# A three-layer transformer on one core: the same program, put in order by another timing model

## The chip, the core and the metric

The kernel runs on one core of a Trainium2 chip. The metric is the device time of one execution in microseconds, lower is better. The core has five engines that work side by side, each on a queue of its own in a fixed order: TensorE (PE for its matmuls, PEld for its weight loads), VectorE (DVE), ScalarE (ACT), GpSimd (POOL) and SyncE (SP), which here only issues transfers.

## What is computed

Three layers run one after the other over 256 tokens of width 1024, all in float32. The first two share a frame and differ in the mixer; the third has a mixer of three parts:

```
for i in range(2):
    x = x + 0.5 * swiglu(rms_norm(x, g[0]), w_gate, w_up, w_down)      # 1024 -> 2816 -> 1024
    x = x + mixer_i(rms_norm(x, g[1]))       # i = 0: gated spatial mixing + a chunked recurrence
                                             # i = 1: attention with low-rank q and k, v (8 heads)
    x = x + 0.5 * swiglu(rms_norm(x, g[2]), w_gate, w_up, w_down)
    x = x + rms_norm(sigmoid(rms_norm(x, g[3]) @ w_gate) * (p_i @ w_proj), g[4])   # embedding layer
x = x + concat(attention, state_space, pooling)(rmsnorm(x)) @ w_out     # hybrid layer
x = x + swiglu(rmsnorm(x), w_gate, w_up, w_down)
return rmsnorm(x)
```

## The kernel before

Activations lie with features on the partitions and the 256 tokens along the free axis; a weight is the stationary operand, 128 by 128, and the activations stream past it in 256 columns. Some products (`tm`) go the other way round, with tokens on the output's partitions and weights as the moving operand, up to 512 columns wide.

A float32 product is made of three passes: every operand is split into a high part in the type that TensorE takes at full pace and a low part, the rest, and high times high, low times high and high times low add up in PSUM. Weights come from HBM packed in pieces of 2048 columns (1 MB), in the order in which the program uses them. `load_piece` (L225) has SP load a piece into one of three buffers, then splits each half of it: ScalarE copies it to `whi` (L248) and VectorE subtracts that from the raw weights into `wlo` (L249). There are six buffers for each of the two parts, so splits can run three pieces ahead. There are 440 pairs of such instructions. All matmuls go through `mm` (L163), so the profile shows nearly all of TensorE under one line.

The program in the order of its stages: `ffn` (the swiglu layers, five of them), `even`, `ple` (the embedding layer, twice), `mla` (attention), `hybrid`, and a last normalization. A normalization needs a sum over features, a matmul with ones (`Stat.begin`), a few tiny VectorE steps (`rsqrt`) and a broadcast by matmul (`Stat.finish`). In `ple` it comes twice: the second one, `now()`, has to be through before the next layer's inputs exist. Behind the first embedding layer, `fill` puts the projection for the second one (`ple_proj`) into that place; behind the second, `fill` is None.

Python only traces the instructions. When the `TileContext` closes, a scheduler puts them in order: it plays the program through on a model of the machine's timing, and whenever an engine is free in that model, gives it the first instruction in program order among those whose inputs and buffers are there by the model's clock. It also hands out the buffers and places all semaphores. The kernel's text steers it in two ways: `high_priority()` moves a block ahead, and `behind(ins)` (the context's `issue_after`) has a block's instructions queued behind a given one on the same engine:

```
m = self.marks if self.hold == 0 else (None, None)
if self.hold == -1:
    m = None, self.rsq
if (self.piece, h) == self.late[0]:
    m = None, self.late[1]
with self.behind(m[0]), self.behind(m[1]):
    nc.scalar.activation(hi[:, i], s, AF.Copy)
    nc.vector.tensor_tensor(lo[:, i], s, hi[:, i].bitcast(FT), op=OP.subtract)
```

On the chip each engine then runs its queue in the order that was fixed at build time, whatever is ready.

In attention (`mla`), the lines that the prediction names: L1001 transposes the rotated key part, L1003 scales it by the keys' norm on VectorE, L936 transposes tiles back through PSUM (once from `big`, once from `o`). In `ple`, L82 and L500 are activations that need another function table than the one before.

Of the kernel before, what the change touches and what calls it, by code (L numbers as in the profile page):

```python
# [1614 lines left out]


def build(nc, a, at):
    with tile.TileContext(nc) as tc, ExitStack() as es:
        k = Kern(nc, tc, a, es, at)
        k.run()  # L1620
    return k.takes
# [19 lines left out]
```

## Time and profile before

| | |
|---|---|
| time, median of 3 runs | 1368.15 us (1366.81 to 1370.12) |
| the profiled execution's own time | 1364.73 us |
| its span, first to last instruction | 1363.0 us |
| instructions | 25969 |
| mean granted TensorE clock | 0.994 |

The profile is of one execution. A row of windows gives, for each engine, the busy time in that stretch and the number of instructions that started there, then the granted clock (1.00 is 2.4 GHz), the share of the DMA engines' time and the bandwidth. A row of the timeline gives start and length in us, engine, line and operands, and in brackets how long the engine sat idle before it and what ended that.

### The profile page before, as it was taken

What the parts mean: (1) busy time and instruction counts of PE and PEld (TensorE: products, weight loads), DVE (VectorE), ACT (ScalarE), POOL (GpSimd) and SP (SyncE); (2) the same over time, 40 slices, a digit from 0 to 9 for tenths busy, and PEclk for the clock granted to TensorE, in tenths of its full rate; (3) what the DMA queues carried; (4) which work ended last, traced back from release to release, by engine and by line L of the source; (5) the groups of instructions that cost most, each with busy time, mean ns of one, the idle gap of its engine ahead of it and who ended that gap; (6) DMA issues with size and microseconds to landing.
All of it is one profiled execution on the core that took longest, in us unless ns stands there. A gap on an engine that the chain in (4) does not pass through costs nothing.

```text
span 1363.0 us, 25969 instructions
## 1 busy us (share of the span) xinstructions
PE 1335.7 (98%) x10872; PEld 1304.9 (96%) x10872; DVE 920.0 (67%) x1527; ACT 726.8 (53%) x1110; POOL 78.3 (6%) x94
## 2 busy tenths in 40 slices
PE   8999999999999999999999899999998999999997
PEld 7999999999999999999999679999998988999997
DVE  6866657968666557866556767766558786766643
ACT  6554546646554456655445656544445665644442
POOL 3100010002000001000010002000001000200001
PEclk9999999999999999999999999999998999999998
DMA  9755555244555453555455323555554442555541
GB/s 323 244 185 183 171 201 173 90 174 168 200 188 203 160 203 138 200 190 188 166 194 193 108 90 132 184 188 188 180 185 156 155 149 100 181 190 187 185 158 60
DMA packets 34645, 235.50 MB, mean 173 GB/s; under 512 B 3984, under 2 KB 4496, under 8 KB 6880
## 3 DMA queue, kind: packets, MB, share of 16 engines
q1 hardware_dynamic: 32976, 230.24, 48.9%
q0 software_dynamic: 832, 2.47, 0.6%
q8 instruction: 85, 1.39, 0.4%
q10 hardware_dynamic: 720, 1.13, 0.2%
q14 instruction: 32, 0.26, 0.1%
HBM read 232.78 MB, written 1.05 MB: 172 GB/s over the span
## 4 chain that ended last, share of the span: by engine, by line
PE 75%; DVE 3%; ACT 2%; issue 1%; DVEq 0%; ACTq 0%
PE acc L163 70%; PE aux L163 5%; DVE wlo L249 1%; PE aux L1119 0%; ACT whi L248 0%; DVE big L1164 0%; DVE qs L950 0%; ACT at L1121 0%; DVE kv L950 0%; ACT ae L1111 0%; ACT big L938 0%; ACT big L1168 0%; DVE big L1486 0%; ACT gu L949 0%; PE aux L936 0%
## 5 line engine op out<-in xcount | busy, mean ns | idle before, releaser
L249 DVE TENSOR_TENSOR wlo<-wraw,whi 128x1024 fp32r<-128x1024 f32 (+1 forms) x440 | 530.8, 1220 | 271.8 <-ACT whi L248 179.8
L248 ACT ACTIVATE whi<-wraw 128x1024 fp32r<-128x1024 f32 (+1 forms) x440 | 451.1, 1047 | 329.0 <-PE acc L163 234.7
L163 PE MATMUL acc<-hh,whi 128*128 128x256 f32 x2192 | 335.0, 283 | 9.0 <-ACT whi L248 5.8
L163 PE MATMUL acc<-hl,whi 128*128 128x256 f32 x2192 | 333.9, 282 | 0.2 <-DVE hl L532 0.2
L163 PE MATMUL acc<-hh,wlo 128*128 128x256 f32 x2192 | 333.1, 282 | 0.7 <-DVE wlo L249 0.7
L163 PEld LDWEIGHTS acc<-hh,whi 128*128 128x128 f32 x2192 | 292.1, 190 | 9.7 <-ACT whi L248 5.8
L163 PEld LDWEIGHTS acc<-hh,wlo 128*128 128x128 f32 x2192 | 292.1, 189 | 1.5 <-DVE wlo L249 1.1
L163 PEld LDWEIGHTS acc<-hl,whi 128*128 128x128 f32 x2192 | 292.2, 189 | 0.4 <-DVE hl L532 0.4
L163 PE MATMUL acc<-big,whi 128*128 128x256 f32 x2032 | 276.1, 282 | 0.0
L163 PEld LDWEIGHTS acc<-big,whi 128*128 128x128 f32 x2032 | 259.7, 188 | 0.4 <-ACT big L259 0.2
L163 PE MATMUL acc<-big,wlo 128*128 128x256 f32 x1016 | 163.6, 282 | 0.0
L163 PEld LDWEIGHTS acc<-big,wlo 128*128 128x128 f32 x1016 | 138.9, 188 | 0.0
L307 POOL TENSOR_TENSOR sqa<-sqa,sq 128x256 f32<-128x256 f32 x72 | 64.0, 889 | 1148.1 <-ACT sq L306 1146.2
L418 DVE TENSOR_TENSOR gu<-acc,rb 128x512 f32<-128x512 f32 (+1 forms) x122 | 81.9, 678 | 56.3 <-PE acc L163 56.3
L262 ACT ACTIVATE hh<-x,cols 128x256 fp32r<-128x256 f32 x64 | 30.2, 503 | 85.2 <-DVE x L457 79.0
L259 ACT ACTIVATE big<-pr 128x256 fp32r<-128x256 f32 x114 | 46.0, 409 | 54.7 <-DVE pr L436 53.0
L434 ACT ACTIVATE sg<-gu 128x256 f32<-128x256 f32 x110 | 44.7, 411 | 37.4 <-DVE gu L418 37.4
L260 DVE TENSOR_TENSOR big<-pr,big 128x256 fp32r<-128x256 f32 x114 | 47.3, 420 | 20.5 <-ACT big L259 20.4
L436 DVE TENSOR_TENSOR pr<-sg,gu 128x256 f32<-128x256 f32 x110 | 45.3, 418 | 3.2 <-ACT sg L434 3.2
L263 DVE SCALAR_TENSOR_TENSOR hl<-x,cols,hh 128x256 fp32r<-128x256 f32 x64 | 37.8, 617 | 8.9 <-ACT hh L262 8.6
L163 PE MATMUL aux<-big 128*128 128x128 f32 (+5 forms) x260 | 39.3, 311 | 0.6 <-DVE big L672 0.6
L306 ACT ACTIVATE sq<-x 128x256 f32<-128x256 f32 x62 | 24.0, 405 | 24.5 <-DVE x L459 18.3
(294 smaller groups left out, 798.3 us busy)
## 6 DMA issues: line engine op xcount, KB each, us to landing
wraw<-wts SPq DMA_DIRECT2D x216, 1024.0 KB, 4.9
wraw<-wts SPq DMA_DIRECT2D x3, 512.0 KB, 8.3
x<-xT SPq DMA_DIRECT2D x3, 256.0 KB, 7.5
wraw<-wts SPq DMA_DIRECT2D x2, 256.0 KB, 3.9
big<-wsT POOLq DMA_DIRECT2D x1, 512.0 KB, 12.6
gu<-pT ACTq DMA_DIRECT2D x2, 256.0 KB, 2.9
out<-big SPq DMA_DIRECT2D x2, 256.0 KB, 2.2
out<-big ACTq DMA_DIRECT2D x2, 256.0 KB, 2.5
```

The lines of the kernel that those rows point to most:

```text
L163: return self.nc.tensor.matmul(out, l, r, start=start, stop=stop, skip_group_check=True).ins
L248: nc.scalar.activation(hi[:, i], s, AF.Copy)
L249: nc.vector.tensor_tensor(lo[:, i], s, hi[:, i].bitcast(FT), op=OP.subtract)
L259: a = nc.scalar.activation(hi, src, AF.Copy)
L260: b = nc.vector.tensor_tensor(lo, src, hi.bitcast(FT), op=OP.subtract)
L262: a = nc.scalar.activation(hi, src, AF.Copy, scale=scale)
L263: b = nc.vector.scalar_tensor_tensor(lo, src, scale, hi.bitcast(FT), op0=OP.mult, op1=OP.subtract)
L306: nc.scalar.activation(q, src, AF.Square)
L307: self.mark = nc.gpsimd.tensor_tensor(self.sq[0], self.sq[0], q, op=OP.add).ins
L418: self.nc.vector.tensor_tensor(out.rearrange("p (u t) -> p u t", u=n), ps.rearrange("p (u t) -> p u t", u=n), rb.unsqueeze(1).to_broadcast ...
L434: self.mark = nc.scalar.activation(sg, gu[:, :T], AF.Silu).ins
L436: nc.vector.tensor_tensor(pr, sg, gu[:, T:], op=OP.mult)
```

## The change

One argument is added where the context is opened. With it the scheduler plays the program through on the build's other timing model, which follows each instruction in more detail. The instructions traced, their priorities, the marks of `behind` and the buffers stay as they are; what may differ is the order in which each engine's queue is filled, and with it which buffer a tile gets and where the semaphores stand.

```
 def build(nc, a, at):
-    with tile.TileContext(nc) as tc, ExitStack() as es:
+    with tile.TileContext(nc, schedule_with_timeline_sim=True) as tc, ExitStack() as es:
         k = Kern(nc, tc, a, es, at)
         k.run()
     return k.takes
```

## Rows read from the trace of the kernel before

**Rows 1.** The page's first part: busy us (share of the span) xinstructions.
```profile
PE 1335.7 (98%) x10872; PEld 1304.9 (96%) x10872; DVE 920.0 (67%) x1527; ACT 726.8 (53%) x1110; POOL 78.3 (6%) x94
```

**Rows 2.** Chain that ended last: by engine (the page), by line (the chain's own view).
```profile
PE 75%; DVE 3%; ACT 2%; issue 1%; DVEq 0%; ACTq 0%
...
by line: PE acc L163 70.0%; PE aux L163 4.9%; DVE wlo L249 0.9%; issue 0.7%; PE aux L1119 0.4%; ACT whi L248 0.3%; DVE big L1164 0.3%; DVE qs L950 0.2%; ACT at L1121 0.2%; DVE kv L950 0.2%; ACT ae L1111 0.2%; ACT big L938 0.2%; ACT big L116
```

**Rows 3.** The page's costliest groups: busy us, mean ns | idle before, releaser.
```profile
L249 DVE TENSOR_TENSOR wlo<-wraw,whi 128x1024 fp32r<-128x1024 f32 (+1 forms) x440 | 530.8, 1220 | 271.8 <-ACT whi L248 179.8
L248 ACT ACTIVATE whi<-wraw 128x1024 fp32r<-128x1024 f32 (+1 forms) x440 | 451.1, 1047 | 329.0 <-PE acc L163 234.7
```

**Rows 4.** Windows by stage, the last one a part of 750:830.
```profile
0.00:25.00 25.00, 18.45 (x137) 18.03 (x138) 16.56 (x31) 15.88 (x30) 12.03 (x22) 1.00 0.87 313
25.00:200.00 175.00, 175.00 (x1468) 175.00 (x1467) 113.19 (x157) 89.15 (x126) 9.20 (x8) 1.00 0.59 201
200.00:300.00 100.00, 99.38 (x755) 93.49 (x754) 80.50 (x139) 57.19 (x74) 2.10 (x3) 1.00 0.45 157
300.00:525.00 225.00, 225.00 (x1910) 224.80 (x1909) 148.74 (x219) 118.91 (x173) 15.94 (x18) 1.00 0.54 185
525.00:550.00 25.00, 23.23 (x194) 22.83 (x193) 20.34 (x42) 16.83 (x33) 1.93 (x3) 1.00 0.25 86
550.00:725.00 175.00, 175.00 (x1488) 175.00 (x1487) 113.52 (x157) 89.18 (x125) 4.41 (x6) 1.00 0.56 193
...
750.00:830.00 80.00, 74.63 (x453) 60.81 (x452) 57.45 (x152) 50.10 (x98) 0.00 (x0) 1.00 0.28 97
830.00:1025.00 195.00, 195.00 (x1657) 194.93 (x1655) 127.75 (x178) 98.83 (x147) 12.59 (x14) 1.00 0.53 184
1025.00:1075.00 50.00, 46.10 (x365) 45.34 (x365) 39.87 (x84) 28.09 (x46) 5.33 (x5) 0.93 0.39 136
1075.00:1150.00 75.00, 74.59 (x551) 66.31 (x551) 60.18 (x158) 50.83 (x97) 0.00 (x0) 1.00 0.40 137
1150.00:1350.00 200.00, 200.00 (x1688) 199.94 (x1688) 121.28 (x168) 98.44 (x144) 12.60 (x13) 1.00 0.48 164
1350.00:1363.00 13.00, 4.27 (x30) 3.80 (x28) 3.73 (x13) 1.04 (x3) 1.41 (x2) 0.67 0.21 81
...
750.00:775.00 25.00, 20.86 (x98) 15.86 (x96) 23.87 (x60) 15.21 (x23) 0.00 (x0) 1.00 0.28 98
```

**Rows 5.** Windows of 5 us behind the second embedding layer.
```profile
1045.00:1050.00 5.00, 2.16 (x11) 1.79 (x12) 3.89 (x12) 1.76 (x6) 0.00 (x0) 0.73 0.57 192
1050.00:1055.00 5.00, 5.00 (x29) 5.00 (x27) 4.86 (x13) 3.27 (x10) 0.00 (x0) 0.59 0.04 18
...
1060.00:1065.00 5.00, 5.00 (x46) 5.00 (x44) 2.19 (x2) 1.76 (x2) 0.00 (x0) 1.00 0.35 95
```

**Rows 6.** Timeline of TensorE at the first embedding layer, of ScalarE at the second.
```profile
538.50 0.51 PE L163 MATMUL acc<-hh,whi 128*128 128x256 f32 x2 [1.57 <-ACT hh L527]
...
1031.87 1.28 ACT L500 ACT_TABLE_LOAD   x1
...
1033.16 1.16 ACT L500 ACTIVATE gu<-gu 128x512 f32<-128x512 f32 x2
```

**Rows 7.** Timeline of VectorE and TensorE in attention, 772 to 777 us.
```profile
773.11 0.38 PE L1001 MATMUL aux<-ident,big 128*128 128x128 f32 x2
773.16 1.22 DVE L249 TENSOR_TENSOR wlo<-wraw,whi 128x1024 fp32r<-128x1024 f32 x1
774.29 1.28 DVE L1003 TENSOR_TENSOR big<-aux,kfr 128x512 f32<-128x512 f32 x2
...
775.13 1.23 PE L936 MATMUL aux<-ident,big 128*128 128x128 f32 x8 [1.64 <-DVE big L1003]
...
776.19 1.04 PE L936 MATMUL aux<-ident,o 128*128 128x128 f32 x8
```

More of the change, by code (lines that the diff above doesn't have):

```diff
@@ L1617, in build @@
 def build(nc, a, at):
-    with tile.TileContext(nc) as tc, ExitStack() as es:
+    with tile.TileContext(nc, schedule_with_timeline_sim=True) as tc, ExitStack() as es:
         k = Kern(nc, tc, a, es, at)
```

## The prediction

> **What bounds the kernel now.** I read the page's engine totals first: TensorE is busy 1335.7 of 1363.0 us [rows 1]. The reader is to see that nothing else comes near it (VectorE is at 920, ScalarE at 727), so an order can only help or harm where TensorE waits. The chain that ended last says the same and names the others: 75% of the span runs through TensorE, 3% through VectorE, 2% through ScalarE, and 0.9% and 0.3% of it are the weight splits of L249 and L248 [rows 2], that is 12.3 and 4.1 us. One such split takes 1.22 us on VectorE and 1.05 us on ScalarE [rows 3], so some ten and four of the 440 pairs stand in that chain today.
>
> The windows by stage then show where TensorE waits [rows 4]. In five long stretches, 970 us together (25:200, 300:525, 550:725, 830:1025, 1150:1350), it is busy without a break; these are the swiglu layers, with VectorE at 61 to 66% and ScalarE at 49 to 53%. Its idle time is elsewhere: 6.55 us at the start, 8.73 at the end, and between them 0.62 in the even mixer (200:300), 1.77 at the first embedding layer (525:550), 5.37 in the attention mixer (750:830), 3.90 at the second embedding layer (1025:1075) and 0.41 in the hybrid layer (1075:1150). The inner five sum to 12.1 us.
>
> **The change part by part.** It adds no operation, removes none and resizes none: same matmuls, same splits, same transfers. What moves is the place of each instruction in its engine's queue. Three kinds of places can move the end.
>
> The swiglu stretches: TensorE never waits in them, and a split (1.22 + 1.05 us) can slide by microseconds under that cover. I cost all reordering there at nothing. Without the cover, one late split of VectorE costs at most its own 1.22 us at each place where it happens. SP's queue holds only the weight loads, in order of the pieces, and its order follows from the buffers; I cost that at nothing too, the DMA share being 0.48 to 0.59 in these stretches.
>
> The stops between layers: the two embedding layers run the same code, but only the first has matmuls of other work (the projection for the next layer) to put under its normalization. The first leaves TensorE idle for 1.77 us, the longest single wait being 1.57 us; the second leaves it idle for 3.90 us [rows 4, 6]. After the second stop the granted clock reads 0.73 and then 0.59, and 29 matmuls start in 5 us where 46 do a little later [rows 5]: (46 - 29) x 5 / 46 = 1.85 us more. So the cover under the first stop is worth 3.90 - 1.77 + 1.85 = 4.0 us. How much of it survives depends on when the scheduler's model thinks that the normalization is due: matmuls that are ready get issued as soon as the model sees TensorE free, and what is issued early covers nothing later. Bounds: nothing lost (0), all lost (+4.0). I take half, +2.0, because nothing in the trace says which way the new model errs.
>
> The latency-bound stretches, attention and hybrid: here a split in the wrong place is paid. At 773.16 us VectorE starts a 1.22 us split; the transposes of L1001 start at 773.11 and last 0.38 us, so L1003 could begin at 773.49 but begins at 774.29, and TensorE waits 1.64 us for it, while the transposes of another tile (ident,o) stand behind in its queue until 776.19 [rows 7]. A different order draws each of these places anew. Bounds: downwards, all the inner idle time of the attention and hybrid stretches, 5.37 + 0.41 = 5.8 us, recovered; upwards, the fourteen splits now in the chain doubled, 16.4 us. I take two more VectorE splits in the chain, 2 x 1.22 = +2.4 us: the gain is capped by what is idle, while every one of the 440 splits is free to land badly, so small errors add up to the slow side.
>
> A rule of the Trainium skill weighs on the cap (page "Perfetto Trace Analysis", section "Identifying the Most-Contended Engine"): matmul busy time is a poor measure of how much TensorE has left, because pipelined matmuls overlap, and the busy share of the weight loads is to be used. By the trace, weight loads are busy 1304.9 us [rows 1], 58.1 us short of the span, of which 41 lie in the five inner stretches [rows 4] against the 12.1 of matmul idle time. By the row of matmuls a perfect order gains 12 us, by the Trainium skill's measure up to 41; part of the difference is no loss at all, since attention's and the even mixer's wide matmuls take longer than their weight loads. The sum above does not use it.
>
> The sum: +2.0 + 2.4 = +4.4 us. The profiled execution took 1364.73 us; the median of the three runs shown is 1368.15, 3.4 us above it. Against the execution that is 1369.1, against the median 1372.6 us. About 0.2%, 2.7 us, is what a measurement of this kernel can tell from no change.
>
> **The rivals.**
>
> *Faster.* The new model puts the chain operations where the hardware can run them. For it: the wait of rows 7, where ready transposes stand behind one that is not; TensorE's idle 5.37 us and its weight loads' idle 19.2 us in 750:830 [rows 4]. Against it: VectorE is nearly without a pause in the first part of it (23.87 of 25 us in 750:775 [rows 4]), and an order cannot shorten its work. Price: half the idle matmul time, 2.7 us, at the least, half of the weight loads' idle time, 9.6, at the most; I take 7, so 1361 us. It decides if TensorE's idle time in 750:830 falls under 3 us with nothing new elsewhere.
>
> *No change that can be measured.* The order differs mainly under cover, or gains and losses cancel: 1368 us. For it speak 970 of 1363 us without any wait. Against it: the other 393 us hold dozens of places at 0.4 to 1.6 us each. This is also the case in which the new model hardly reorders at all.
>
> *Much slower.* In the three stretches where VectorE is busiest (80.5% of 200:300, 72% of 750:830, 80% of 1075:1150 [rows 4]) splits reach VectorE late, and TensorE, whose queue stops at the first matmul that isn't ready [rows 7], waits for the low part of a weight tile. If each of the three loses, beyond today, about what attention shows today (5.37 us), and one of them is followed by a fall of the clock (1.85), that is 3 x 5.37 + 1.85 = 18 us: 1386 us. Against it: six buffers for each part of a split let them run three pieces ahead.
>
> *The pace.* The unbroken stretches do not run at one pace: 1468 matmuls in 175 us (25:200) but 1488 in 175 us (550:725), for the same kind of layer and at the same clock of 1.00 [rows 4]. All 970 us hold 8211; at the best pace they would take 965.7 us (4.3 less), at the worst 978.8 (8.8 more). I see no cause for it in these views; if it hangs on the order, it outweighs the rest: 1364 to 1377 us.
>
> *Table loads.* ScalarE's order also sets how often it reloads its function table, 1.28 us each [rows 6]. Three more in the chain would be +3.8 us; this is inside the likeliest case's range. The Trainium skill's page "ScalarE: Activation LUTs", section "What ACT_TABLE_LOAD costs", puts a switch at 2.66 us with its drain, which would make three of them 8 us; the trace does not agree, as the table load at 1031.87 us, 1.28 us long, is followed by its activation at 1033.16 [rows 6].
>
> **How the numbers follow.** Slightly slower, as summed: 0.33, with its own range 1370.9 to 1380. Faster: 0.31. No change: 0.20. Much slower: 0.10. The pace: 0.06, half to each side. So faster 0.34, same 0.20, slower 0.46, and the time of the likeliest is 1372.6 us. The range of 8 in 10 reaches down through most of the faster case (1361, with 5 us below it for the upper bound of its gain) to 1356, and up to 1390, which holds the much slower case at its price and leaves out its far end.
>
> **What would show it.** Right: TensorE's idle time at the first embedding layer rises from 1.77 towards 3.9 us, with a clock below 1.00 behind it; the chain's share of L249 rises above 0.9%; the five unbroken stretches stay unbroken. Wrong: the idle time in 750:830 falls well below 5.4 us; or idle time appears inside a swiglu layer, which I cost at nothing; or the number of matmuls per 25 us in unbroken stretches moves as a whole.

## The result, and the profile after

The changed kernel takes 1403.25 us (median of four runs, 1399.57 to 1403.33), the kernel before 1367.48 us beside it (1366.74 to 1370.12): a ratio of 1.0261 [1.0239, 1.0283], 2.6% slower. The prediction said 1372.6 us. The profiled execution took 1403.33 us, 1401.6 of them the span, at a mean granted clock of 0.981 (0.994 before).

First the page of the changed kernel, the lines that answer to [rows 1 to 3].

```profile
PE 1350.4 (96%) x10872; PEld 1318.1 (94%) x10872; DVE 925.1 (66%) x1527; ACT 729.8 (52%) x1112; POOL 70.7 (5%) x94
...
PE 90%; DVE 6%; ACT 2%; issue 1%; DMA 1%; POOL 0%; SPq 0%; DVEq 0%; ACTq 0%; POOLq 0%
PE acc L163 84%; PE aux L163 5%; DVE wlo L249 2%; ACT whi L248 1%; DMA wraw<-wts 1%; PE aux L936 1%; PE aux L1119 0%; DMA x<-xT 0%; DVE hl L263 0%; ACT hh L262 0%; POOL sqa L307 0%; ACT sq L306 0%; ACT ae L1111 0%; DVE big L658 0%; DVE x L410 0%
...
L249 DVE TENSOR_TENSOR wlo<-wraw,whi 128x1024 fp32r<-128x1024 f32 (+1 forms) x440 | 527.3, 1215 | 311.4 <-ACT whi L248 205.3
```

The work is the same: equal counts on TensorE, VectorE and GpSimd, two more table loads on ScalarE (its count went from 1110 to 1112). What grew is waiting. TensorE's matmul idle time went from 27.3 to 51.2 us (span less busy time), +23.9 of the span's +38.6; the rest is busy time that grew by 14.7, at a lower mean clock. VectorE stood idle ahead of its splits for 311.4 us, 40 more than before [rows 3]. Its splits' share of the chain went from 0.9% [rows 2] to 2%, but the two shares can't be compared as they stand: the chain of before can be followed back only to 249.3 us (so its shares by engine sum to 81%), the new one to 0.7 us. From 250 us on, the splits of L249 are 12.1 us of the chain before and 21.0 after.

The windows by stage, which answer to [rows 4], show where; the stages lie later than before by what the stages ahead of them lost. Columns: length; busy time and count of PE, PEld, DVE, ACT, POOL; granted clock; DMA share; GB/s.

```profile
25.00:50.00 25.00, 23.43 (x199) 23.25 (x198) 21.82 (x33) 15.48 (x24) 1.63 (x2) 1.00 0.86 302
50.00:275.00 225.00, 225.00 (x1813) 220.61 (x1812) 151.78 (x217) 121.75 (x157) 6.49 (x9) 1.00 0.52 182
275.00:325.00 50.00, 44.85 (x361) 42.76 (x360) 32.95 (x65) 24.18 (x45) 5.83 (x7) 0.97 0.29 101
325.00:525.00 200.00, 200.00 (x1700) 200.00 (x1700) 130.34 (x192) 100.40 (x140) 6.25 (x9) 1.00 0.54 188
525.00:575.00 50.00, 47.89 (x391) 47.31 (x390) 40.04 (x73) 32.01 (x52) 4.09 (x5) 0.97 0.39 141
...
750.00:875.00 125.00, 114.66 (x748) 100.46 (x747) 86.76 (x205) 71.67 (x135) 5.74 (x7) 0.96 0.32 110
875.00:1050.00 175.00, 175.00 (x1478) 175.00 (x1477) 108.26 (x150) 83.19 (x118) 5.47 (x7) 1.00 0.54 187
1050.00:1100.00 50.00, 45.00 (x343) 44.41 (x342) 41.42 (x77) 28.53 (x48) 5.12 (x5) 0.90 0.38 129
1100.00:1150.00 50.00, 45.68 (x342) 42.98 (x341) 35.89 (x85) 33.16 (x54) 0.00 (x0) 0.97 0.48 167
1150.00:1225.00 75.00, 66.84 (x498) 60.04 (x498) 49.25 (x112) 36.69 (x71) 5.83 (x7) 0.90 0.28 99
```

The reader is to see that the swiglu stretches are as unbroken as before, and that the idle time is in the even mixer's end (5.2 us in 275:325), in attention (10.3 in 750:875) and above all in the hybrid layer (4.3 in 1100:1150, 8.2 in 1150:1225), where it had been 0.4 [rows 4]. The second embedding layer (1050:1100) has 5.0, where it had 3.9. The lower clock is in the same places, and at the first embedding layer (525:575).

Since the stages shift, I cut both executions by the number of matmuls started (every order has the same 10872, and at these counts the same ones lie behind). Times between the cuts, in us, from the starts of the matmuls in the traces, one execution of each kernel; the last three columns are runs told below:

```
matmuls       what lies there           before  after  pe_new_all  pe_old_all  three_stretches
0-220         start                       35.0   36.2        38.8        38.9             36.5
220-1900      swiglu                     205.8  204.6       204.5       203.7            203.5
1900-2700     even mixer                 100.3  107.1       101.0       112.2            100.8
2700-6050     swiglu, embedding, swiglu  397.3  400.1       400.7       399.8            399.7
6050-7400     attention, swiglu          186.8  196.7       190.8       199.6            189.0
7400-8200     swiglu                      94.5   94.9        94.6        95.0             95.0
8200-9400     embedding, hybrid          159.0  177.7       177.2       176.8            158.9
9400-10871    swiglu                     177.1  177.0       177.0       175.5            176.6
```

Of the 38.5 us by which the last matmul starts later, 18.7 are in the hybrid's stretch, 9.9 in attention's, 6.8 in the even mixer's: 35.4 in three places. The hybrid's stretch also holds the second embedding layer: of its 18.7, 16.0 lie between the 8750th and the 9020th matmul (34.7 us before, 50.7 after), where the hybrid's state matmuls are, 1.9 at the embedding layer's stop (8380 to 8420) and 1.5 behind the hybrid (9230 to 9400). The first row differs by up to 3 us between executions with the same order there (36.2 here, 39.0 in splits_and_keys below), so its 1.2 shows nothing. What TensorE waited for, by the view of waits over the whole execution (us in total, times, longest):

```profile
PE aux L163 <- DVE big L1308: 8.5, 2, 4.3
...
PE aux L936 <- DVE big L992: 4.3, 1, 4.3
...
PE acc L163 <- DVE big L418: 2.8, 1, 2.8
PE aux L163 <- DVE big L705: 2.6, 1, 2.6
...
PE acc L163 <- DVE gu L418: 1.9, 2, 1.6
```

L1308 is the last VectorE step before the hybrid's state matmuls, L992 scales attention's keys, L705 is the even mixer's level step. None of the waits that are new is for a weight split (one of 5.8 us for L248, at the start, is the same in the kernel before). The timeline shows why they are long. TensorE in the hybrid:

```profile
1138.94 1.50 PE L163 MATMUL aux<-ident,ac 128*128 128x128 f32 x12
1140.20 0.84 PE L163 MATMUL acc<-whi,hl 128*128 128x256 f32 x5
1140.88 1.12 PE L163 MATMUL acc<-wlo,hh 128*128 128x256 f32 x8
...
1142.43 0.28 PE L163 MATMUL acc<-o,wlo 128*128 128x256 f32 x1
1146.87 1.54 PE L163 MATMUL aux<-big 128*64 128x256 f32 x4 [4.16 <-DVE big L1308]
1148.34 2.72 PE L163 MATMUL aux<-ident,ac 128*128 128x128 f32 x12
...
1156.15 2.80 PE L163 MATMUL aux<-big 128*64 128x256 f32 x12 [4.29 <-DVE big L1308]
```

and VectorE beside its first wait:

```profile
1140.33 0.86 DVE L1303 TENSOR_SCALAR big<-aux,ac 128x128 f32<-128x128 f32 x3
1142.19 0.35 DVE L1305 TENSOR_SCALAR ae<-aux,ac 128x128 f32<-128x128 f32 x1 [1.00 <-ACT big L1304]
1142.46 2.35 DVE L249 TENSOR_TENSOR wlo<-wraw,whi 128x1024 fp32r<-128x1024 f32 x2
1144.72 0.34 DVE L1305 TENSOR_SCALAR ae<-aux,ac 128x128 f32<-128x128 f32 x1
1145.50 0.35 DVE L1305 TENSOR_SCALAR ae<-aux,ac 128x128 f32<-128x128 f32 x1 [0.43 <-ACT big L1304]
1145.77 0.95 DVE L1308 TENSOR_TENSOR big<-big 128x768 f32<-128x768 f32 x1
```

Each broadcast (`ident,ac`) starts a chain on VectorE and ScalarE that ends in L1308 some 8 us later (1138.94 to 1146.72 by the rows). Behind the first, TensorE has 19 matmuls of other work left (5, 8 and the six of `o`), and idles 4.16 us; behind the second it has only eight small ones, which finish the states before, and idles 4.29. The matmuls that could have stood there, the projections into `acc`, had all been run ahead of the broadcasts. And two splits stand in VectorE's part of the chain. The same two things, cover spent early and splits inside a chain, are the theories of the experiments.

The start shows the first of them in its smallest form: the normalization's broadcast (2 matmuls) is queued behind 39 matmuls of the first swiglu layer instead of ahead of them, and TensorE idles 1.6 us until VectorE has scaled the first product with it (L418 above; 1.57 us in 25:50, where it was busy throughout before).

### The profile page after: what moved, and what is told of

It reads as the page before. It is cut to its first block, busy times and chain, and to the rows that moved or that the text cites. A ratio compares the mean times of both kernels' runs of the same rounds, so it can differ in the third digit from the quotient of the medians.

```text
span 1401.6 us, 26020 instructions
## 1 busy us (share of the span) xinstructions
PE 1350.4 (96%) x10872; PEld 1318.1 (94%) x10872; DVE 925.1 (66%) x1527; ACT 729.8 (52%) x1112; POOL 70.7 (5%) x94
## 4 chain that ended last, share of the span: by engine, by line
PE 90%; DVE 6%; ACT 2%; issue 1%; DMA 1%; POOL 0%; SPq 0%; DVEq 0%; ACTq 0%; POOLq 0%
PE acc L163 84%; PE aux L163 5%; DVE wlo L249 2%; ACT whi L248 1%; DMA wraw<-wts 1%; PE aux L936 1%; PE aux L1119 0%; DMA x<-xT 0%; DVE hl L263 0%; ACT hh L262 0%; POOL sqa L307 0%; ACT sq L306 0%; ACT ae L1111 0%; DVE big L658 0%; DVE x L410 0%
## 5 line engine op out<-in xcount | busy, mean ns | idle before, releaser
L249 DVE TENSOR_TENSOR wlo<-wraw,whi 128x1024 fp32r<-128x1024 f32 (+1 forms) x440 | 527.3, 1215 | 311.4 <-ACT whi L248 205.3
L248 ACT ACTIVATE whi<-wraw 128x1024 fp32r<-128x1024 f32 (+1 forms) x440 | 452.3, 1049 | 387.9 <-PE acc L163 297.5
L307 POOL TENSOR_TENSOR sqa<-sqa,sq 128x256 f32<-128x256 f32 x72 | 59.6, 828 | 1190.0 <-ACT sq L306 1187.9
L418 DVE TENSOR_TENSOR gu<-acc,rb 128x512 f32<-128x512 f32 (+1 forms) x122 | 81.7, 678 | 54.5 <-PE acc L163 54.2
L263 DVE SCALAR_TENSOR_TENSOR hl<-x,cols,hh 128x256 fp32r<-128x256 f32 x64 | 43.7, 709 | 13.7 <-ACT hh L262 13.6
L163 PE MATMUL aux<-big 128*128 128x128 f32 (+5 forms) x260 | 41.9, 334 | 11.1 <-DVE big L1308 8.5
L163 PEld LDWEIGHTS aux<-big 128*128 128x128 f32 (+2 forms) x260 | 31.2, 195 | 17.8 <-ACT ae L1307 8.8
```

The lines of the kernel that those rows point to most:

```text
L163: return self.nc.tensor.matmul(out, l, r, start=start, stop=stop, skip_group_check=True).ins
L263: b = nc.vector.scalar_tensor_tensor(lo, src, scale, hi.bitcast(FT), op0=OP.mult, op1=OP.subtract)
L307: self.mark = nc.gpsimd.tensor_tensor(self.sq[0], self.sq[0], q, op=OP.add).ins
L418: self.nc.vector.tensor_tensor(out.rearrange("p (u t) -> p u t", u=n), ps.rearrange("p (u t) -> p u t", u=n), rb.unsqueeze(1).to_broadcast ...
```

## The experiments

The two builds differ in order alone: 1618 of TensorE's 10578 places, 729 of VectorE's 1527, 371 of ScalarE's 1065 (the profile has more records, 10872 for TensorE and 1110 for ScalarE before, than their queues have places); GpSimd's and SyncE's queues are the same. So the edit of nearly every run is to give some queue, or a stretch of it, a stated order, and to leave the rest to the scheduler with one or the other model:

```diff
+def pin(tc, nc, engine, runs):
+    """Have these instructions of an engine (by their place in the trace) queued in this order."""
+    mine = [i for i in nc.cur_bb.bb.instructions if i.engine == engine and not isinstance(i, mybir.BassTileRelease)]
+    order = [mine[r] for first, n in runs for r in range(first, first + n)]
+    info = mybir.DependencyInfo(mybir.DependencyClass.NoSync, mybir.DependencyReason.DATA)
+    for before, after in zip(order, order[1:]):
+        tc.add_manual_dep(after, before.name, info, reason="pin")
...
         k.run()
+        pin(tc, nc, mybir.EngineType.PE, ORDER_0)
```

`ORDER_n` lists the instructions by their place in the program's text; below, only the engines and stretches are named. The ratios are to the kernel before, run beside each. The changed kernel's own VectorE and ScalarE queues beside all of TensorE's queue of before, and the reverse, were not run.

### One engine's queue at a time

**pe_old_all**: the new model, TensorE's whole queue as before. The scheduler then draws VectorE's and ScalarE's anew.

> Context opened with the new model, but TensorE's queue held to the order of the kernel before, all 10578 matmuls of it; VectorE's and ScalarE's orders are still drawn by the new model. Theory 1 (the new model lets matmuls that could cover a wait go ahead of the chain that they should cover, so the loss is in TensorE's order): 1366 to 1376 us. Theory 2 (the loss is in VectorE's and ScalarE's orders, weight splits ahead of chain operations): it stays at 1395 us or above.

Measured: 1410.30 us, 1.0298 [1.0269, 1.0327]. **pe_new_all**: the old model, TensorE's whole queue as in the changed kernel.

> The reverse: context opened with the old model, TensorE's queue held to the order of the changed kernel, VectorE's and ScalarE's orders drawn by the old model. Theory 1: 1394 to 1408 us. Theory 2: 1372 us or less.

Measured: 1390.54 us, 1.0162 [1.0134, 1.0190]. **pe_old_hybrid** and **pe_old_mla**: the new model, TensorE's queue as before in the hybrid's (686 places) or attention's (448) stretch alone.

> New model, TensorE's queue held to the old order in the hybrid layer alone (686 matmuls). Theory 1: TensorE's idle time from 1125 to 1225 us, 12.5 us in the changed kernel, falls below 3, the clock there stays at 1.00, and the time is 1384 to 1392 us. Theory 2: 1399 us or more.

Measured: 1398.68 us, 1.0227 [1.0205, 1.0248].

> New model, TensorE's queue held to the old order in the attention mixer alone (448 matmuls). Theory 1: its idle time, 10.3 us in the changed kernel against 5.4 before, falls back to about 5.4, and the fall of the clock there goes: 1391 to 1398 us. Theory 2: 1400 us or more.

Measured: 1405.88 us, 1.0260 [1.0227, 1.0293], no different from the changed kernel.

The first theory, that the loss is TensorE's order, fell as it was put: giving TensorE its old order back made things no better, yet giving the kernel before the new one cost 22 us. The second fell with it: it allowed pe_new_all 1372 us at the most. The table shows what each did. With the new TensorE order alone (pe_new_all) the hybrid's stretch takes 177.2 us, all of its loss; attention's 4.0 of its 9.9; the even mixer's 0.7 of 6.8. With the old TensorE order among the new VectorE and ScalarE queues (pe_old_all), the even mixer's stretch is worse than in the changed kernel. In pe_old_hybrid the waits for L1308 are gone and another one stands in the hybrid's stretch, for ScalarE's L1168:

```profile
PE aux L1274 <- ACT big L1168: 4.4, 1, 4.4
```

TensorE now reaches the transposes (L1274) early, as it did before; the likely reason for the wait, which no run isolates, is that the operations ahead of them are queued on the other engines for a TensorE that comes late.

### All three queues, one stretch at a time

Next theory (A): the loss is local to three stretches, and the three queues of a stretch belong together. The rival (B): it comes from what the rest of the program hands over. All are the changed kernel with TensorE, VectorE and ScalarE queued as before in the stretch named.

> The changed kernel, with TensorE, VectorE and ScalarE queued as before in the stretch of the hybrid layer alone (1050 to 1225 us); the rest as the new model orders it. Theory A (the loss is local: each stretch loses what its own three queues cost it, and gets that back when all three are as before): the stretch between the 8200th and the 9400th matmul was 159.0 us before and 177.8 after, so 1403 - 18.8, 1382 to 1388 us. Theory B (a stretch's loss comes from what the rest of the program hands to it, as pinning TensorE's order alone suggested when it moved the idle time to other places): less than half of it, 1394 us or more.

Measured: 1383.21 us, 1.0110 [1.0092, 1.0128].

> The changed kernel, with the three queues as before in the latent attention's stretch alone (750 to 875 us). Theory A: the stretch between the 6050th and the 7400th matmul was 186.8 us before and 196.6 after, so 1403 - 9.8, 1391 to 1396 us. Theory B: 1398 us or more.

Measured: 1396.25 us, 1.0212 [1.0192, 1.0232].

> The changed kernel, with the three queues as before in the even layer's stretch alone (200 to 350 us). Theory A: the stretch between the 1900th and the 2700th matmul was 100.3 us before and 107.1 after, so 1403 - 6.8, 1394 to 1399 us. Theory B: 1400 us or more.

Measured: 1395.50 us, 1.0193 [1.0176, 1.0211].

> The three before together: the three queues as before in the even, latent attention and hybrid stretches, and the new model's order in all the rest. Theory A: 18.8 + 9.8 + 6.8 = 35.4 back of 1403, 1366 to 1372 us; what is left over before is the start and the two embedding layers. Theory B: 1380 us or more.

Measured: 1369.11 us, 1.0003 [0.9991, 1.0016], the time of the kernel before. Theory A holds (three_mla lies 0.25 us above its range, less than its interval). From the ratios, the three give back 20.6, 6.7 and 9.3 us ((1.0261 - 1.0110) x 1367.5, and so on), 36.6 in sum, and together 35.3 of 35.7. Outside the three stretches the new order is worth nothing that can be measured, either way. TensorE at the hybrid's second broadcast, in three_hybrid:

```profile
1136.74 1.60 PE L163 MATMUL aux<-ident,ac 128*128 128x128 f32 x12
1138.11 0.60 PE L163 MATMUL acc<-hl,whi 128*128 128x256 f32 x3
1138.54 0.75 PE L163 MATMUL acc<-hh,wlo 128*128 128x256 f32 x5
...
1140.02 1.56 PE L163 MATMUL acc<-hh,wlo 128*128 128x256 f32 x11
1141.41 1.12 PE L163 MATMUL acc<-whi,hh 128*128 128x256 f32 x8
...
1145.70 0.65 PE L163 MATMUL aux<-big 128*64 128x256 f32 x4
```

Here 54 fill matmuls (3, 5, 11, four times 8 and 3, all into `acc`) lie between the broadcast and the next state matmuls at 1145.70, and TensorE idles nowhere. In the changed kernel there are none. The state matmuls start 9.0 us after the broadcast here, 7.8 there: the chain is no shorter, it is covered. Nor is it free of splits. VectorE in the same stretch of three_hybrid:

```profile
1141.56 1.22 DVE L249 TENSOR_TENSOR wlo<-wraw,whi 128x1024 fp32r<-128x1024 f32 x1
...
1142.95 1.21 DVE L249 TENSOR_TENSOR wlo<-wraw,whi 128x1024 fp32r<-128x1024 f32 x1
...
1144.35 0.95 DVE L1308 TENSOR_TENSOR big<-big 128x768 f32<-128x768 f32 x1
```

The good order has two splits ahead of L1308 as well, and they cost nothing under that cover.

**two_as_before**: the changed kernel with VectorE and ScalarE as before in the three stretches and TensorE's order left to the new model, the mirror of pinning TensorE alone.

> The changed kernel with VectorE and ScalarE queued as before in the three stretches and TensorE as the new model has it beside them. Theory C: the hybrid's loss stays (about 15 us between the 8800th and the 9150th matmul), the even layer's and half of the attention's come back (there the kernel before with the changed kernel's TensorE order lost 0.6 of 6.8 and 4.1 of 9.8 us): 1403 - 12, 1388 to 1394 us. Theory S: nearly everything comes back, 1368 to 1376 us.

Measured: 1406.81 us, 1.0294 [1.0274, 1.0313]. Neither expectation held: not even the even mixer's loss came back (its cuts at 1900 and 2700 are 109.6 us apart). The hybrid's stretch got back 4.8 of its 18.7 us (172.9), and attention's took 198.8. Two queues of the good order beside a third of the other gave nothing in all.

### Cover spent early (theory C)

**cover_early**: the old model, with TensorE's queue of the changed kernel in 158 places of the hybrid.

> The kernel before, under its own model, with TensorE queued as in the changed kernel in the hybrid's state and pooled attention matmuls alone (158 places of 10578; VectorE and ScalarE follow in 34 and 16 places). Theory C: the fill matmuls stand ahead of the two states' broadcasts again, and the stretch between the 8800th and the 9150th matmul goes from 47.4 towards the 62.9 us of the changed kernel: 1368 + 10 to 16, 1378 to 1384 us. Theory S: VectorE's splits stand as before, at most +4, 1368 to 1372 us.

Measured: 1371.83 us, 1.0036 [1.0023, 1.0050]. The expectation named the wrong place: the 158 are the pooled attention's matmuls, behind the states'. Its order costs 4.9 us, with new waits for L1115 (1.6 us) and L418 (0.8). So two more runs took the right ones.

> The kernel before, under its own model, with TensorE queued as in the changed kernel from the hybrid's transposes (L1274) to the end of its states' matmuls (204 places, the stretch from about the 8810th to the 9010th matmul; the run named cover_early had taken the pooled attention behind it). VectorE and ScalarE follow in 93 and 43 places. Theory C (fill spent ahead of the chain): most of the hybrid's loss, +9 to +15, 1377 to 1383 us, with two idle stretches of about 4 us before states' matmuls that wait for L1308. Theory D (the loss needs VectorE's and ScalarE's new orders too): at most +4, 1368 to 1372 us.

Measured: 1380.46 us, 1.0109 [1.0084, 1.0135]. **hybrid_pe_new** takes TensorE's new order over the hybrid's whole stretch.

> The kernel before with TensorE queued as in the changed kernel in the whole hybrid stretch. Theory C: the stretch between the 8200th and the 9400th matmul as in the run with all of the changed kernel's TensorE order, 177 against 159 us, +17 to +19, 1384 to 1388 us. Theory D: 1368 to 1374 us.

Measured: 1385.55 us, 1.0138 [1.0116, 1.0159]. Theory C holds for the hybrid: 204 places of TensorE's queue, under the old model, cost 14.9 us, and the whole stretch 18.9. (VectorE and ScalarE, drawn by the old model around them, followed in the 93 and 43 places that the expectation names.) The waits of states_early in the hybrid are led by the changed kernel's:

```profile
PE aux L163 <- DVE big L1308: 7.9, 2, 4.1
```

### Splits and other work inside a chain (theory S)

**splits_behind**: all three queues as in the changed kernel, but for 12 of VectorE's 440 splits, queued a few places later. (The expectation's first count, 11, is a slip; its list has 12.)

> The changed kernel with all three queues as they are in it, but for 11 of VectorE's weight splits (L249) in the three stretches, which are queued some places later, behind the chain operations that they stand ahead of: one behind the even layer's last level operations (L705 to L721), two behind its L810 and L263, two behind the attention's L992, two behind the query's rsqrt steps, two behind softmax divisions (L1116), and three of the hybrid's behind L1230 and L1310 (12 in all, 1.2 us each). Theory S (the loss is splits standing in the chains, the rival of the prediction): the chains lose 12 x 1.2 us and the waits in front of them, 10 us or more come back, 1385 to 1393 us. Theory C (the loss is matmuls that covered the chains, queued ahead of them and gone when the chain comes): a split that leaves the chain shortens idle time only where the chain ends last, 1 to 6 us, 1397 to 1402 us.

Measured: 1398.13 us, 1.0238 [1.0219, 1.0257]; its interval overlaps the changed kernel's, and it lies in the range given to theory C. By the cuts, the even mixer's stretch gives back 3.9 us, the hybrid's 2.3, and attention's loses 3.1, where the wait for L1115, in the query's softmax, went from 2.2 to 4.3 us. In the even mixer the split stood right in front of what TensorE waited for. VectorE and TensorE of the changed kernel there:

```profile
277.03 1.21 DVE L249 TENSOR_TENSOR wlo<-wraw,whi 128x1024 fp32r<-128x1024 f32 x1
...
278.49 0.69 DVE L705 TENSOR_TENSOR big<-big 128x512 f32<-128x512 f32 x1
...
279.33 8.00 PE L163 MATMUL aux<-big 128*128 128x128 f32 x64 [2.63 <-DVE big L705]
```

Attention was to be the clearest case: two splits between the steps of the keys' reciprocal square root, and 4.33 us of idle time behind them. VectorE and TensorE of the changed kernel:

```profile
778.82 0.17 DVE L280 TENSOR_SCALAR nb<-kv 128x16 int32<-128x16 int32 x1
...
779.47 1.23 DVE L249 TENSOR_TENSOR wlo<-wraw,whi 128x1024 fp32r<-128x1024 f32 x1
...
780.70 1.22 DVE L249 TENSOR_TENSOR wlo<-wraw,whi 128x1024 fp32r<-128x1024 f32 x1
...
784.56 2.36 DVE L992 TENSOR_TENSOR big<-big,kfn 128x1024 f32<-128x1024 f32 x2
...
785.93 3.37 PE L936 MATMUL aux<-ident,big 128*128 128x128 f32 x16 [4.33 <-DVE big L992]
```

With both moved away, in splits_behind, the wait stayed: 4.09 us. TensorE and VectorE of that run:

```profile
778.77 3.53 PE L936 MATMUL aux<-ident,big 128*128 128x128 f32 x16 [4.09 <-DVE big L992]
...
773.96 0.69 DVE L950 TENSOR_REDUCE qs<-gu 128x4 f32<-128x512 f32 x1 [1.07 <-ACT gu L949]
775.34 0.69 DVE L950 TENSOR_REDUCE qs<-gu 128x4 f32<-128x512 f32 x1 [0.69 <-ACT gu L949]
775.95 0.17 DVE L284 TENSOR_TENSOR nz<-ny 128x16 f32<-128x16 f32 x1
```

Two sums of the *query's* squares also stand in the keys' chain, and those wait for ScalarE, which waits for TensorE. The splits had filled time in which VectorE waits once they are gone. So the next runs moved everything: the two splits, three sums (L950) and a rope step (L1033).

> The changed kernel, all queues as they are in it, but for six VectorE operations of the attention that are queued behind the keys' last scaling (L992): two splits, a rope operation (L1033) and three sums of the query's squares (L950). With the splits alone behind it the idle time before L992's transposes stayed at 4.3 us, and two sums, which wait for ScalarE and TensorE, set the time of the chain. Theory K (the keys' chain is late because the query's operations stand ahead of it in VectorE): idle 4.3 to under 1.5 us there, 3 to 5 us back, 1398 to 1400 us. Theory Q (the query's chain then ends last): the idle time moves to L1115, total unchanged, 1402 to 1404 us.

Measured: 1401.81 us, 1.0259 [1.0236, 1.0281]. The six operations now stood between L992 and L1003, the next step of the same chain, and the wait moved there. The waits in the attention of keys_first have

```profile
PE aux L936 <- DVE big L1003: 3.0, 1, 3.0
```

With five of the six behind L1003 too, in **keys_whole**, this is

```profile
PE aux L936 <- DVE big L1003: 0.9, 1, 0.9
```

> As the run named keys_first, but five of the six VectorE operations (two splits, three sums) are queued behind the keys' second scaling too (L1003); in keys_first they had stood between L992 and L1003, L992 started 3.8 us earlier, and TensorE's idle time moved from L992 (4.3 us) to L1003 (3.0). Theory K: both idle stretches fall under 1 us, 3 to 5 us back, 1398 to 1400 us. Theory Q: the query's sums are then late, the idle time moves to the query's softmax (L1115), 1402 to 1404 us.

Measured: 1397.44 us, 1.0226 [1.0197, 1.0254]. The wait for L992 is gone, and the query did not become late (L1115: 2.2 us in both). The interval touches the changed kernel's; by the cuts at 6050 and 6600, attention is 3.0 us shorter.

> The changed kernel with three sets of VectorE operations queued later: the even layer's three splits and the hybrid's two at L1310 from the run named splits_behind (4.0 and 2.5 us back there), and the attention's six of keys_whole. Theory K with additive parts: 1403 - 4.0 - 2.5 - 3.5, 1391 to 1395 us. Theory Q, or parts that spoil one another: 1396 to 1400 us.

Measured: 1390.46 us, 1.0177 [1.0151, 1.0203]: eleven of VectorE's 1527 instructions in other places, the two other queues untouched, are 11.5 us, clear of the changed kernel's interval. By the cuts 3.9 are the even mixer's and 3.6 attention's (up to 6600); the hybrid's wait for L1308 fell by only 1.0 us (8.5 to 7.5), since ScalarE's L1304 ends last once the splits are gone. The rest of the 11.5 can't be placed: the traced execution, at 1395.26 us, is the slowest of the six.

### Can the kernel before be improved the same way?

**chain_first**: the kernel before, with nine VectorE operations moved out of attention's chains.

> The kernel before with its three queues as they are, but for nine VectorE operations of the latent attention queued later: five behind the keys' L992 and L1003 (three splits and two sums of the query), two splits behind the keys' L979 to L1030, two behind the query's first softmax steps. In the kernel before TensorE idles 0.9 us for L992, 1.6 for L1003, 1.1 and 0.6 near L1030. If a split ahead of a chain costs what TensorE idles behind it: 2 to 4 us less, 1364 to 1366 us. If the chain's length there is covered or its end is set by something else: 1368 us, and slower if the splits' own matmuls then wait.

Measured: 1368.32 us, 1.0008 [0.9995, 1.0022], no gain. The wait for L1003 fell from 1.6 to 0.9 us, and the one for L1115 rose from 0.3 to 1.4. There the query's chain ends last next. No version here beats the kernel before.

## Why the prediction was wrong

The direction was the likeliest one given; the size was off by 30.7 us. Two of its three signs of being right came true all the same: the chain has more of L249, and the five stretches stayed unbroken. Neither tells 4 us from 36, and none of its signs looked at the hybrid.

**The swiglu stretches at nothing: right.** They stay unbroken, and their cuts agree within 3 us each. The pace did not move as a whole: 1700 matmuls in 200 us and 1478 in 175 are 212.5 and 211.1 per 25 us, between the two paces of before (209.7 and 212.6 in [rows 4]). That rival is out.

**The first embedding layer, +2.0: not borne out.** TensorE idles 2.1 us in 525:575 against 1.77, but at the stop itself (between the cuts at 4250 and 4500) it idles 1.78 us against 1.77; the other 0.3 is a small wait behind it. These cuts are 33.2 us apart against 32.0, because the clock fell there. That is not the order's doing: chain_first, with TensorE's queue of before, has the fall too (33.2), and splits_behind, with the changed kernel's, has not (31.8). So the cover survived, the lower bound that the prediction gave. The cover that was lost is at the second embedding layer, where it put nothing: 3.9 us of idle time became 5.0.

**The latency-bound stretches, +2.4: this is the step that failed.** "I take two more VectorE splits in the chain" measured 35.3 us, the three stretches together. In its own unit it did not even rise: from 250 us on, the chain passes through 12.1 us of VectorE splits in attention's and the hybrid's stretches before, and 8.4 after; the rise to 21.0 is in the even mixer (7.9) and in the stretch behind it (4.8). Three things were wrong with it. It priced single instructions, when whole groups of TensorE's matmuls had changed places with a chain: that alone is 14.9 to 18.9 us in the hybrid. It had the right mechanism one paragraph earlier ("what is issued early covers nothing later") and applied it only to the embedding layer; the hybrid's 0.41 us of idle time [rows 4] entered only as what could be gained, and the upper bound, 16.4 us, counted splits alone. But the idle time was small *because* the cover fitted: in the kernel before, as in three_hybrid, 54 matmuls lie between the second broadcast (1113.40) and the state matmuls that need it (1122.36), and the program's text has a projection between the two groups of states. And the even mixer (0.62 us idle) was left out of this term altogether; there splits did stand in the chain, and three of them moved gave back 3.9 us.

**The clock.** The +1.85 us for one fall was counted at one place. In the changed kernel it falls behind most of the new stops; windows of 5 us in the hybrid:

```profile
1145.00:1150.00 5.00, 3.13 (x12) 2.22 (x13) 1.75 (x4) 0.89 (x2) 0.00 (x0) 0.73 0.64 210
...
1155.00:1160.00 5.00, 3.85 (x18) 2.27 (x19) 2.46 (x6) 0.52 (x1) 0.00 (x0) 0.50 0.00 0
```

0.50 is the lower of the two levels, 1.2 of 2.4 GHz: the twelve broadcast matmuls that took 1.50 us at 1138.94 take 2.72 at 1148.34. Over the execution TensorE was busy for 40.2 us at the lower level, by the trace's clock, and for 6.5 before. If the same work takes half the time at the upper level, as about in these twelve matmuls, the falls cost 17 us more than before, an estimate; the busy time grew by 14.7. About two fifths of the loss is this. Most of it lies behind the stops; two of the falls (at 546 and 758 us, 3.4 us each) come and go between executions of one order.

**The rivals.** *Much slower* (1386 us, 0.10) named the three stretches rightly and the clock, but had another mechanism: splits that come late, with TensorE waiting for a weight's low part. The waits of the changed kernel have none of these. Where splits cost something, as in the even mixer, they come *early* and hold up a chain behind them, and VectorE waits 40 us more ahead of them than before. Splits are the smaller part: with the other chain work moved with them, 11.5 of 35.8 us. *Faster* is out: idle time in 750:875 rose from 5.4 to 10.3 us. *No change* is out. *Table loads* are out too: the two more (L609 and L623, at 236.0 and 239.9 us) stand in the even mixer, where the chain that ended last is TensorE's own matmuls from 213.1 to 256.1 us, and the time of loads in that chain is 2.4 us against 2.9 before.

The Trainium skill's measure that the prediction weighed (page "Perfetto Trace Analysis", section "Identifying the Most-Contended Engine": judge TensorE by its weight loads' busy share rather than the matmuls') adds little here: their idle time grew by 25.4 us (58.1 to 83.5), that of the matmuls by 23.9, of a span that grew by 38.6. Neither shows which part of the busy time ran at the lower clock.

What stays open: the part of attention's 9.9 us beyond the keys' chain (3 to 3.6) and TensorE's order (4.0), which may overlap, and the even mixer's beyond the three splits (they gave back 3.9 of 6.8). Why the more detailed model draws this order was not studied; on the chip only its effect was.

## What to carry to other kernels

An idle time near zero in a stretch that holds a long chain does not say that little can be lost there: ask how long the chain is and how many matmuls hide it, and price the worst case of a new order by the chain's whole length, once for each pass, with a fall of the clock behind each stop. In a new order look first at what stands between the start of a chain and its end on every queue: fill should stand behind the matmul that starts the chain, and splits and sums of other chains behind its last step. The orders of the engines belong together: part of a good order put beside queues drawn anew gave nothing back in pe_old_all and two_as_before (1.0298 and 1.0294, against 1.0261), and what moved as a unit is a stretch with all its queues (1.0003).

## What had not been expected of the hardware

Work that fills a wait gives nothing back when it is taken out: two splits of 1.2 us inside the keys' chain were taken out and the chain ended no earlier, because the next instruction of VectorE's queue waited 1.07 and 0.69 us for ScalarE instead. And TensorE loses twice at a stop: of the 16.0 us between the 8750th and the 9020th matmul, 11.1 are idle time (8.5 for L1308, 2.8 for L418), and 4.9 are growth of the busy time, 10.8 us of which ran at the clock of 0.50, so that the hybrid's loss is more than its waits.
